# adaLN quarters of the first stage moved ahead of the latents' products of the round before

## The chip, the cores and the metric

The kernel runs on one core of a Trainium2 chip. A core has five engines that run side by side, each through a list of instructions in a fixed order: TensorE (PE) multiplies matrices, VectorE (DVE) and ScalarE (ACT) work on elements, GpSimd (POOL) has little to do here, and SyncE (SP) issues the loads from memory, which 16 DMA engines carry out. The metric is the device time of one launch in microseconds (us), as the median of several runs.

## The reference

The program is a decoder trunk of two layers for 256 tokens of width 1024, in float32. Each sub-layer is normalised, scaled and shifted by vectors that come from a conditioning vector c (adaLN). Only the start of the first layer matters here: the modulation, the normalisation and the first projection of the latent attention.

```python
cond = jax.nn.silu(c)
for i in range(DEPTH):
    mod = cond @ ada_w[i] + ada_b[i]
    sh1, sc1, g1, sh2, sc2, g2 = [m[:, None, :] for m in jnp.split(mod, N_MOD, axis=-1)]
    h = rms_norm(x, norm_mix[i]) * (1.0 + sc1) + sh1
    # layer 0: latent attention
    proj = h @ w_in                                  # 1024 x (512 + 256 + 32)
    q_lat, kv_lat, k_rope = jnp.split(proj, [Q_LORA, Q_LORA + KV_LORA], axis=-1)
    q = (rms_norm(q_lat, q_norm) @ w_qb)
    kv = (rms_norm(kv_lat, kv_norm) @ w_kvb)
```

The gates, the dense feed-forward layer, the gated delta layer and the experts come after that, in the same way in both kernels.

## The kernel before

**Halves.** Products are made from float32 numbers cut in two: a high half in a reduced format and the rest. A weight slab is loaded by a DMA into one of 10 ring tiles (`wload`, L182; tile `w`), copied into its high half by ScalarE (CAST, tile `whi`, L463) and the rest is found by VectorE (subtraction, tile `wlo`, L468); `Flow.split` (L454) issues both. There are four tiles for `whi` and four for `wlo`. Each block product is three matmuls: high by high, high by low, low by high (L885 to L887), so the third reads `wlo`.

**Stage and rounds.** The first stage works in four rounds (i = 0 to 3, `mla`, L871). Round i treats a quarter of the model width, 256 columns, which is two of the eight blocks of 128. The shift sh1 and the scale sc1 of these columns are made by an adaLN quarter: 4 loads of 512 KB (`ada_load`, L630; those of h = 1 of quarter 3 go to a pool of their own, tile `adaw`), two halves of 8 products each with the conditioning vector as stationary operand (`ada_half`, L647, products at L652; the profile counts 16 instructions), a copy from PSUM by VectorE (`adarow`, L657), two transposes (L659), and then, on VectorE, column sums (`half`, `mod`, `scl`, L664 to L668). `norm_blocks` (L373) then writes the two blocks of the normalised input: `nt` (VectorE, L378), its high half `hhi` (ScalarE, L382), its low half `hlo` (VectorE, L389).

The latents' weights of a round are two slabs, 288 KB for kv (with the rotary key) and 512 KB for q. `latents(i, "kv")` makes 18 products from the first slab, `latents(i, "q")` 24 from the second (`latents`, L877), all summed in PSUM banks over the four rounds.

**Order.** The order on TensorE, VectorE, ScalarE and GpSimd is the order in which the program calls; nothing reorders it. SP's order is the order of `loads` with `load_to` (L643), where a load waits until its ring tile is free and until the load eight places earlier has landed. In a round the kernel before splits the round's two slabs first, then makes the two halves of the quarter, and weaves the products of the round before between them: kv behind the first half, q behind the quarter's transposes. Between the rounds VectorE works at the tables of the rotary embedding (`rope_steps`, nine steps at a time). After the fourth round come the products of round 3, then the latents' own norms (`ss`, `r`) and the projections to heads. The name k0 stands for the first slab of those (slab 8 of the flow), q0 for the next (slab 9).

Of the kernel before, what the change touches and what calls it, by code (L numbers as in the profile page):

```python
# [23 lines left out]
AHEAD = 6  # L24
# [25 lines left out]
def hybrid_kernel(ctx: ExitStack, tc: tile.TileContext, rope_rows, x, c, positions, ada_w, ada_b,  # L50
# [31 lines left out]
    def acc_bank(name="acc"):  # L82
        return banks["pool"].tile([128, 512], F32, name=name, tag="acc", bufs=banks["acc"])
# [88 lines left out]
    def rope_steps(n):  # L172
        for _ in range(n):
            next(rope, None)
# [7 lines left out]
    def wload(srcs, shape, name="w"):  # L182
        raw = (ring[0]() if ring else wrw).tile(shape, F32, name=name, tag="w")
        for dst, src in srcs(raw):
            nc.sync.dma_start(dst, src)
        return raw
# [177 lines left out]
    def in_rows(r, bank):  # L364

        pb = bank("rb")
        for t in range(2):
            nc.tensor.transpose(pb[:, t * 128:(t + 1) * 128], r[:, t:t + 1].to_broadcast([128, 128]), ident)
        return pb[:, :S]
# [3 lines left out]
    def norm_blocks(layer, which, blocks, r, hi, lo, share=(), depth=1):  # L373
        late = []
        for i in blocks:
            t = sm.tile([128, S], F32, name="nt", tag="sq", bufs=4)
            sh = modT[layer, 3 * which][:, i:i + 1]
            nc.vector.scalar_tensor_tensor(t, in0=xT[:, i, :], scalar=scl[layer, which][:, i:i + 1],  # L378
                                           in1=r, op0=OP.mult, op1=OP.mult)
            if len(late) == depth:  # L380
                late.pop(0)()
            nc.scalar.activation(hi[:, i, :], t, AF.Identity, bias=sh)  # L382

            def low(i=i, t=t, sh=sh):
                if i in share:
                    nc.scalar.activation(t, t, AF.Identity, bias=sh)
                    nc.gpsimd.tensor_tensor(lo[:, i, :], t, hi[:, i, :].bitcast(F32), op=OP.subtract)
                else:
                    nc.vector.scalar_tensor_tensor(lo[:, i, :], in0=t, scalar=sh, in1=hi[:, i, :].bitcast(F32),  # L389
                                                   op0=OP.add, op1=OP.subtract)  # L390

            late.append(low)
        for low in late:
            low()
# [177 lines left out]
    for t in range(2):  # L572
        q = sm.tile([128, D], F32, name="xsq", tag="xsq", bufs=1)
# [37 lines left out]
    for name in GROUPS_T:  # L611
        t, i = int(name[1]), len(slabs)
# [10 lines left out]
    flow = Flow(slabs, uses, lambda i: False, 3)  # L623
# [4 lines left out]
    ada_raw, loads = {}, []  # L628

    def ada_load(i, h, m):  # L630
        wv = ada_w[0].rearrange("(k p) c -> p k c", p=128)[:, 4 * h:4 * h + 4, m * D + i * S:m * D + (i + 1) * S]
        if (i, h) == (3, 1):
            raw = adp.tile([128, D], F32, name="adaw", tag="w").rearrange("p (k c) -> p k c", k=4)
            nc.sync.dma_start(raw, wv)
        else:
            raw = wload(lambda t: [(t, wv)], [128, 4, S])
        ada_raw[i, h, m] = raw

    for i in range(4):
        loads += [lambda i=i, h=h, m=m: ada_load(i, h, m) for h in range(2) for m in range(2)]  # L640
        loads += [lambda j=j: flow.load(j) for j in (2 * i, 2 * i + 1)]

    def load_to(n):  # L643
        while 24 - len(loads) < n:
            loads.pop(0)()

    def ada_half(i, h, ps):  # L647
        for k in range(4):
            for m in range(2):
                kk = 4 * h + k  # L650
                c = 64 * m + 32 * (k % 2)
                mm(ps[c:c + 32, :S], lhsT=csil[:, kk:kk + 1].to_broadcast([128, 32]),  # L652
                   rhs=ada_raw[i, h, m][:, k, :], start=kk < 2, stop=kk > 5, tile_position=(0, c))

    def ada_quarter(i, ps):
        row = adp.tile([128, S], F32, name="adarow", tag="row", bufs=1)
        nc.vector.tensor_copy(row, ps[:, :S])  # L657
        for cc in range(2):
            nc.tensor.transpose(ps[:, S + cc * 128:S + (cc + 1) * 128], row[:, cc * 128:(cc + 1) * 128], ident)  # L659
        c = slice(2 * i, 2 * i + 2)  # L660
        pv = ps[:, S:].rearrange("p (c m j r) -> p m c j r", c=2, m=2, j=2)[:, :, :, :, 0]
        for m in (1, 0):
            half = sm.tile([128, 2], F32, name="half", tag="half", bufs=2)
            nc.vector.tensor_tensor(half, pv[:, m, :, 0], adab[:, 0, m, c], op=OP.add)  # L664
            nc.vector.tensor_tensor(modT[0, m][:, c], pv[:, m, :, 1], half, op=OP.add)
            if m == 1:
                g = cols[:, col_of["nm"] + 2 * i:col_of["nm"] + 2 * i + 2]
                nc.vector.scalar_tensor_tensor(scl[0, 0][:, c], in0=modT[0, 1][:, c], scalar=1.0, in1=g,  # L668
                                               op0=OP.add, op1=OP.mult)
        norm_blocks(0, 0, (2 * i, 2 * i + 1), rx, hhi, hlo)  # L670
# [195 lines left out]
    def room(name):  # L866
        while waiting[0] > 2:
            flow.idle()
        return mm_bank(name)

    def mla():  # L871
# [5 lines left out]
        def latents(i, which):  # L877
            flow.begin()
            for k, (h, l) in enumerate(flow.slab[2 * i + (which == "q")]):
                kk = 2 * i + k  # L880
                rh, rl = hhi[:, kk, :], hlo[:, kk, :]
                for j, (bank, b) in enumerate(place[which]):
                    o = bank[:, b * S:(b + 1) * S]
                    c = slice(160, 288) if which == "kv" and j == 2 else slice(j * 128, (j + 1) * 128)
                    mm(o, lhsT=h[:, c], rhs=rh, start=kk == 0 and b == 0, stop=False, skip_group_check=True)  # L885
                    mm(o, lhsT=h[:, c], rhs=rl, start=False, stop=False, skip_group_check=True)
                    mm(o, lhsT=l[:, c], rhs=rh, start=False, stop=kk == 7, skip_group_check=True)  # L887
            flow.advance()

        load_to(10)  # L890
        for i in range(4):
            flow.split(True)
            flow.split(True)
            load_to(min(24, 12 + 6 * i))
            ps = ada_bank[i % 2]
            for h in range(2):
                ada_half(i, h, ps)
                if i == h == 0:
                    nc.scalar.copy(rx, in_rows(xr, acc_bank))
                load_to(min(24, 14 + 6 * i + 2 * h))  # L900
                if i == 3 and h:
                    flow.load(9)
                    flow.ahead = AHEAD
                    flow.split(True)
                if h:
                    ada_quarter(i, ps)
                if i:
                    latents(i - 1, ("kv", "q")[h])
            rope_steps(9)

        def out_of(which, j):
            bank, b = place[which][j]
            return bank[:, b * S:(b + 1) * S]
# [24 lines left out]
        for name in GROUPS_T:  # L938
            t, i = int(name[1]), at[name]
            if name[0] == "k":  # L940
                ps = room("k")
# [8 lines left out]
                ps = room("v")  # L950
# [12 lines left out]
            else:  # L963
                for u in range(3):
                    ps = room("qr") if u == 0 else ps if u == 2 else room("q")
# [52 lines left out]
    for i, _ in enumerate(mla()):  # L1018
        if i > 4:
            next(pair, None)  # L1020
# [42 lines left out]
    flow = ffn_flow  # L1063
# [133 lines left out]
    flow = gdn_flow  # L1197
# [521 lines left out]
    ps = acc_bank("pos")  # L1719
# [511 lines left out]
```

## Time and profile before

| | us |
|---|---|
| median of 3 runs | 995.1 (992.34 to 997.79) |
| the profiled execution | 997.03 |
| its span, first to last instruction | 995.3 |
| TensorE busy | 931.6 (94%) |
| VectorE busy | 671.4 (67%) |
| ScalarE busy | 486.2 (49%) |
| mean granted clock of TensorE | 0.963 of full speed |

Times in the trace count from the start of the span. A row of the timeline is one instruction or a run of equal ones; in square brackets stand how long its engine had been idle before it and what released it. Matmuls are pipelined, so the distance of their starts says more than their durations: 0.28 us is the duration of a product of 256 columns, but the next one starts 0.12 us later. The granted clock is a share of TensorE's full 2.4 GHz; it is either 0.5 or 1, and a stretch in between mixes both. The DMA share is the mean busy share of the 16 DMA engines; packets overlap, so it can pass 1.

### The profile page before, as it was taken

How to read it: one execution, taken by the hardware profiler on the slowest of the kernel's cores; microseconds unless marked ns; L12 is line 12 of the kernel's file. 1: busy time of each engine (PE TensorE's matmuls, PEld its weight loads, DVE VectorE, ACT ScalarE, POOL GpSimd, SP SyncE). 2: the span in 40 equal slices, each digit the busy share in tenths (PEclk: the TensorE clock that was granted, in tenths of full speed). 3: DMA queues.
4: the chain of work that ended last, by engine and by line, in shares of the span. 5: the costliest groups of instructions: out<-in, count | busy, mean ns of one | idle time of the engine just before them, and what ended most of it. 6: DMA issues, size and time to landing. Idle time of an engine off the chain costs nothing. (4 is left out here: it accounts for less than half of the span.)

```text
span 995.3 us, 18930 instructions
## 1 busy us (share of the span) xinstructions
PE 931.6 (94%) x6802; PEld 749.5 (75%) x6802; DVE 671.4 (67%) x1281; ACT 486.2 (49%) x877; POOL 123.7 (12%) x226
## 2 busy tenths in 40 slices
PE   5899999999999999899999989899989999999995
PEld 3787888999999989789889877755774567356642
DVE  5778957877777768977764458925872488257532
ACT  2366646444444457544563366723662366236422
POOL 2000001000000024535663240000000000000000
PEclk7999998999999989899999979999999999999998
DMA  9959995979988955432223365979999999999992
GB/s 308 366 178 315 303 288 167 312 238 338 312 285 293 304 163 179 140 107 86 86 86 101 113 212 175 318 259 370 365 394 370 363 353 342 382 358 367 364 372 71
DMA packets 152741, 261.34 MB, mean 263 GB/s; under 512 B 13650, under 2 KB 104832, under 8 KB 152640
## 3 DMA queue, kind: packets, MB, share of 16 engines
q1 hardware_dynamic: 152336, 259.81, 76.3%
q8 instruction: 55, 0.90, 0.4%
q0 software_dynamic: 304, 0.25, 0.1%
q14 instruction: 46, 0.38, 0.1%
HBM read 258.97 MB, written 1.05 MB: 261 GB/s over the span
## 5 line engine op out<-in xcount | busy, mean ns | idle before, releaser
L463 ACT CAST whi<-w 128x1024 fp32r<-128x1024 f32 (+3 forms) x147 | 138.6, 958 | 115.4 <-PE gu L1145 45.0
L200 DVE TENSOR_TENSOR wlo<-w,whi 128x1024 fp32r<-128x1024 f32 (+1 forms) x136 | 153.0, 1155 | 33.8 <-ACT whi L199 32.1
L468 DVE TENSOR_TENSOR wlo<-w,whi 128x1024 fp32r<-128x1024 f32 (+3 forms) x132 | 147.9, 1135 | 21.6 <-ACT whi L463 21.2
L199 ACT CAST whi<-w 128x1024 fp32r<-128x1024 f32 (+1 forms) x136 | 131.8, 998 | 35.7 <-PE gu L2069 18.5
L1144 PE MATMUL gu<-hhi,whi 128*128 128x256 f32 x336 | 95.4, 284 | 0.0
L1146 PE MATMUL gu<-hhi,wlo 128*128 128x256 f32 x336 | 95.1, 283 | 0.0
L1145 PE MATMUL gu<-hlo,whi 128*128 128x256 f32 x336 | 95.1, 283 | 0.0
L2099 PE MATMUL gu<-w,XF 128*64 128x512 f32 (+1 forms) x384 | 85.3, 564 | 0.0
L232 PE MATMUL pj<-hhi,whi 128*128 128x256 f32 x240 | 73.6, 307 | 0.0
L234 PE MATMUL pj<-hhi,wlo 128*128 128x256 f32 x240 | 68.5, 286 | 3.8 <-DVE wlo L468 3.8
L233 PE MATMUL pj<-hlo,whi 128*128 128x256 f32 x240 | 68.4, 285 | 0.0
L468 POOL TENSOR_TENSOR wlo<-w,whi 128x1024 fp32r<-128x1024 f32 x15 | 39.3, 2622 | 226.3 <-DVE al L1119 181.2
L1145 PEld LDWEIGHTS gu<-hlo,whi 128*128 128x128 f32 x336 | 64.5, 192 | 0.0
L1144 PEld LDWEIGHTS gu<-hhi,whi 128*128 128x128 f32 x336 | 64.5, 192 | 0.0
L1146 PEld LDWEIGHTS gu<-hhi,wlo 128*128 128x128 f32 x336 | 64.5, 192 | 0.0
L2069 PE MATMUL gu<-whi,XH 128*128 128x512 f32 x192 | 59.4, 390 | 3.6 <-ACT whi L199 3.4
L2069 PE MATMUL gu<-wlo,XH 128*128 128x512 f32 x192 | 59.7, 392 | 2.2 <-DVE wlo L200 2.2
L2099 PEld LDWEIGHTS gu<-w,XF 128*64 128x64 f32 x384 | 26.4, 136 | 44.5 <-issue 39.5
L2069 PE MATMUL gu<-whi,XL 128*128 128x512 f32 x192 | 58.2, 385 | 0.0
L262 DVE SCALAR_TENSOR_TENSOR adacc<-adaw,csil,adacc 128x1024 f32<-128x1024 f32 x42 | 56.1, 1336 | 2.2 <-DMA adaw<-in_ada_w_dram 2.2
L1106 PE MATMUL acc<-ah,whi 128*128 128x256 f32 x176 | 50.0, 284 | 0.0
L1107 PE MATMUL acc<-al,whi 128*128 128x256 f32 x176 | 49.8, 283 | 0.0
(526 smaller groups left out, 2213.0 us busy)
## 6 DMA issues: line engine op xcount, KB each, us to landing
w<-in_moe_w_down_dram SPq DMA_DIRECT2D x84, 512.0 KB, 6.8
w<-in_moe_w_gate_up_dram SPq DMA_DIRECT2D x128, 256.0 KB, 5.4
w<-in_moe_w_gate_up_dram SPq DMA_DIRECT2D x64, 512.0 KB, 6.9
adaw<-in_ada_w_dram SPq DMA_DIRECT2D x50, 512.0 KB, 5.3
w<-in_moe_w_gate_up_dram SPq DMA_DIRECT2D x128, 192.0 KB, 4.0
w<-in_ada_w_dram SPq DMA_DIRECT2D x46, 512.0 KB, 6.6
w<-in_ffn_w_gate_up_dram SPq DMA_DIRECT2D x88, 256.0 KB, 5.5
w<-in_gdn_w_in_dram SPq DMA_DIRECT2D x32, 512.0 KB, 4.6
```

Of the source, the lines that this page charges most:

```text
L199: nc.scalar.copy(dv(hi), rv(raw))
L200: eng.tensor_tensor(dv(lo), rv(raw), dv(hi).bitcast(F32), op=OP.subtract)
L232: mm(ps, lhsT=lhi, rhs=rhi, start=first, stop=False)
L233: mm(ps, lhsT=lhi, rhs=rlo, start=False, stop=False)
L234: mm(ps, lhsT=llo, rhs=rhi, start=False, stop=last)
L463: nc.scalar.copy(dv(hi), rv(raw))
L468: eng.tensor_tensor(dv(lo), rv(raw), dv(hi).bitcast(F32), op=OP.subtract)
L1144: mm(o, lhsT=h[:, c], rhs=rh, start=k == g == 0 and new, stop=False, skip_group_check=True)
L1145: mm(o, lhsT=h[:, c], rhs=rl, start=False, stop=False, skip_group_check=True)
L1146: mm(o, lhsT=l[:, c], rhs=rh, start=False, stop=k == 1 and g == 3, skip_group_check=True)
L2069: mm(p[:, :2 * m].rearrange("p (g c) -> p g c", g=2), lhsT=x[:, kk, :], rhs=w[:, k, :, o:o + m], start=kk == i == 0, stop=kk == 7 and i == 2)
L2099: mm(o, lhsT=X[:, k, :], rhs=r, start=k == 0, stop=k == 7, tile_position=(0, 64 * h))
```

## The change

The list of loads is written out: quarter 0, weights 0, quarter 1, quarter 2, weights 1, quarter 3, weights 2, weights 3, where before each quarter was followed by the weights of its own round. The split of a pair of slabs moves too. Weights 0 are split at the start; weights 1 behind quarter 2, weights 2 behind quarter 3, weights 3 after the loop. The products of the round before no longer stand between the halves of a quarter (but for kv of round 0, which stays between the halves of quarter 1): in rounds 2 and 3 both halves and the transposes come first, then the split, then kv and q. The split of k0 and the loads ahead of it move from the middle of round 3 to after the loop.

```diff
-    for i in range(4):
-        loads += [lambda i=i, h=h, m=m: ada_load(i, h, m) for h in range(2) for m in range(2)]
-        loads += [lambda j=j: flow.load(j) for j in (2 * i, 2 * i + 1)]
+    for what, i in (("a", 0), ("w", 0), ("a", 1), ("a", 2), ("w", 1), ("a", 3), ("w", 2), ("w", 3)):
+        if what == "a":
+            loads += [lambda i=i, h=h, m=m: ada_load(i, h, m) for h in range(2) for m in range(2)]
+        else:
+            loads += [lambda j=j: flow.load(j) for j in (2 * i, 2 * i + 1)]
...
         load_to(10)
-        for i in range(4):
+
+        def weights():
             flow.split(True)
             flow.split(True)
+
+        weights()
+        for i in range(4):
             load_to(min(24, 12 + 6 * i))
             ps = ada_bank[i % 2]
             for h in range(2):
...
                 load_to(min(24, 14 + 6 * i + 2 * h))
-                if i == 3 and h:
-                    flow.load(9)
-                    flow.ahead = AHEAD
-                    flow.split(True)
-                if h:
-                    ada_quarter(i, ps)
-                if i:
-                    latents(i - 1, ("kv", "q")[h])
+                if i == 1 and h == 0:
+                    latents(0, "kv")
+            ada_quarter(i, ps)
+            if i > 1:
+                weights()
+                latents(i - 1, "kv")
+            if i:
+                latents(i - 1, "q")
             rope_steps(9)
+        weights()
+        flow.load(9)
+        flow.ahead = AHEAD
+        flow.split(True)
```

TensorE around quarter 2, before: the end of the kv products of round 1, the second half of the quarter, its transposes, and the q products of round 1. The names in brackets are semaphores, DMAHW those of loads, DVE and Activation those of VectorE and ScalarE.

```order
L885 MATMUL lat<-hhi,whi 128x256
L886 MATMUL lat<-hlo,whi 128x256
L887 MATMUL lat<-hhi,wlo 128x256
L652 MATMUL ada<-w,csil 32x256 [waits DMAHW0_49]
L652 MATMUL ada<-w,csil 32x256 [waits DMAHW1_49]
L652 MATMUL ada<-w,csil 32x256 x6
L659 MATMUL ada<-ident,adarow 128x128 [waits DVE_49]
L659 MATMUL ada<-ident,adarow 128x128
L885 MATMUL lat<-hhi,whi 128x256
L886 MATMUL lat<-hlo,whi 128x256
L887 MATMUL lat<-hhi,wlo 128x256
```

The same place after: the last products before it are those of q of round 0, and behind the transposes stand kv of round 1.

```order
L889 MATMUL lat<-hhi,wlo 128x256
L654 MATMUL ada<-w,csil 32x256 [waits DMAHW4_49]
L654 MATMUL ada<-w,csil 32x256 [waits DMAHW5_49]
L654 MATMUL ada<-w,csil 32x256 x6
L654 MATMUL ada<-w,csil 32x256 [waits DMAHW6_49]
L654 MATMUL ada<-w,csil 32x256 [waits DMAHW7_49]
L654 MATMUL ada<-w,csil 32x256 x6
L661 MATMUL ada<-ident,adarow 128x128 [waits DVE_49]
L661 MATMUL ada<-ident,adarow 128x128
L887 MATMUL lat<-hhi,whi 128x256 [waits Activation_49]
L888 MATMUL lat<-hlo,whi 128x256
L889 MATMUL lat<-hhi,wlo 128x256 [waits DVE_49]
```

Both halves now stand together, and the first and the third product behind the transposes wait for ScalarE and VectorE, where before none of them waited.

VectorE around quarter 2, before: weights 2 are split ahead of the quarter's `adarow`, weights 3 behind its `hlo`.

```order
L468 TENSOR_TENSOR wlo<-w,whi 128x576 [waits DMAHW2_49,Activation_49]
L468 TENSOR_TENSOR wlo<-w,whi 128x1024 [waits DMAHW3_49,PE_49,Activation_49]
L657 COPY adarow<-ada 128x256 [waits PE_49]
L664 TENSOR_TENSOR half<-ada,adab 128x2 [waits PE_49]
L665 TENSOR_TENSOR mod_125<-ada,half 128x2 [waits DVE_49]
L668 SCALAR_TENSOR_TENSOR scl_136<-mod_125,cols 128x2 [waits DVE_49]
L664 TENSOR_TENSOR half<-ada,adab 128x2
L665 TENSOR_TENSOR mod_124<-ada,half 128x2 [waits DVE_49]
L378 SCALAR_TENSOR_TENSOR nt<-xT,scl_136,rx 128x256 x2
L389 SCALAR_TENSOR_TENSOR hlo<-nt,mod_124,hhi 128x256 [waits Activation_49] x2
L468 TENSOR_TENSOR wlo<-w,whi 128x576 [waits DMAHW0_49,Activation_49]
L468 TENSOR_TENSOR wlo<-w,whi 128x1024 [waits DMAHW1_49,PE_49,Activation_49]
```

The same place after: the quarter, and behind it the split of weights 1.

```order
L659 COPY adarow<-ada 128x256 [waits PE_49]
L666 TENSOR_TENSOR half<-ada,adab 128x2 [waits PE_49]
L667 TENSOR_TENSOR mod_125<-ada,half 128x2 [waits DVE_49]
L670 SCALAR_TENSOR_TENSOR scl_136<-mod_125,cols 128x2 [waits DVE_49]
L666 TENSOR_TENSOR half<-ada,adab 128x2
L667 TENSOR_TENSOR mod_124<-ada,half 128x2 [waits DVE_49]
L378 SCALAR_TENSOR_TENSOR nt<-xT,scl_136,rx 128x256 x2
L389 SCALAR_TENSOR_TENSOR hlo<-nt,mod_124,hhi 128x256 [waits Activation_49] x2
L468 TENSOR_TENSOR wlo<-w,whi 128x576 [waits DMAHW0_49,Activation_49]
L468 TENSOR_TENSOR wlo<-w,whi 128x1024 [waits DMAHW1_49,Activation_49]
```

The rows are the same instructions in the same order, but the subtraction behind the quarter is now that of the slabs whose products stand next on TensorE.

## Rows read from the trace of the kernel before

**Rows 1.** Stretches: us, busy time of each engine, granted clock, DMA share, GB/s

```profile
15.00:25.00 10.00, 8.05 (x55) 3.68 (x48) 8.61 (x24) 3.57 (x6) 0.00 (x0) 0.50 1.09 356
...
30.00:35.00 5.00, 5.00 (x50) 4.28 (x49) 3.87 (x13) 1.88 (x5) 0.00 (x0) 1.00 1.08 359
...
55.00:60.00 5.00, 5.00 (x47) 5.00 (x45) 3.40 (x15) 3.48 (x10) 0.00 (x0) 1.00 0.34 129
```

**Rows 2.** Timeline of TensorE, end of the stage: start, us, instruction [idle before]

```profile
55.15 0.28 PE L887 MATMUL lat<-hhi,wlo 128*128 128x256 f32 x1
55.27 0.95 PE L344 MATMUL ss<-ones,lsq 128*128 128x1 f32 x8
```

**Rows 3.** Timeline of round 1, TensorE and VectorE

```profile
27.11 1.07 PE L652 MATMUL ada<-w,csil 128*32 128x256 f32 x16
27.45 1.89 DVE L468 TENSOR_TENSOR wlo<-w,whi 128x576 fp32r<-128x576 f32 x2
...
29.25 0.42 DVE L657 COPY adarow<-ada 128x256 f32<-128x256 f32 x1
...
29.73 0.44 PE L659 MATMUL ada<-ident,adarow 128*128 128x128 f32 x2 [1.55 <-DVE adarow L657]
```

**Rows 4.** Timeline of round 2, TensorE, VectorE and ScalarE

```profile
36.30 1.07 PE L652 MATMUL ada<-w,csil 128*32 128x256 f32 x16
...
37.69 0.42 DVE L657 COPY adarow<-ada 128x256 f32<-128x256 f32 x1
...
38.16 0.44 PE L659 MATMUL ada<-ident,adarow 128*128 128x128 f32 x2 [0.80 <-DVE adarow L657]
...
38.68 0.28 PE L887 MATMUL lat<-hhi,wlo 128*128 128x256 f32 x1
...
39.88 0.91 ACT L382 ACTIVATE hhi<-nt,mod 128x256 fp32r<-128x256 f32 x2 [3.36 <-DVE nt L378]
...
40.42 0.89 DVE L389 SCALAR_TENSOR_TENSOR hlo<-nt,mod,hhi 128x256 fp32r<-128x256 f32 x2 [0.18 <-ACT hhi L382]
...
40.69 0.66 ACT L463 CAST whi<-w 128x576 fp32r<-128x576 f32 x1
...
41.38 0.76 DVE L468 TENSOR_TENSOR wlo<-w,whi 128x576 fp32r<-128x576 f32 x1
...
42.01 1.05 ACT L463 CAST whi<-w 128x1024 fp32r<-128x1024 f32 x1 [0.66 <-DMA w<-in_mla_w_in_dram]
...
43.09 1.23 DVE L468 TENSOR_TENSOR wlo<-w,whi 128x1024 fp32r<-128x1024 f32 x1 [0.95 <-ACT whi L463]
```

**Rows 5.** Timeline of round 3, VectorE and TensorE

```profile
45.42 1.29 DVE L468 TENSOR_TENSOR wlo<-w,whi 128x512 fp32r<-128x512 f32 x2 [1.10 <-ACT whi L463]
...
47.11 0.44 PE L659 MATMUL ada<-ident,adarow 128*128 128x128 f32 x2 [1.30 <-DVE adarow L657]
```

**Rows 6.** Waits from 15 to 56 us (total, times, longest); stretches from the start

```profile
PEld ada L652 <- issue: 1.8, 7, 0.3
...
0.00:30.00 30.00, 16.89 (x109) 10.59 (x109) 18.34 (x55) 8.38 (x13) 6.54 (x19) 0.77 0.98 315
...
0.00:40.00 40.00, 26.09 (x198) 18.28 (x199) 25.78 (x78) 11.90 (x20) 6.54 (x19) 0.83 1.00 326
```

**Rows 7.** Timeline of TensorE behind the stage, and the clock there

```profile
59.17 1.84 PE L344 MATMUL ss<-ones,lsq 128*128 128x1 f32 x16
63.32 0.40 PE L368 MATMUL rb<-ident,r 128*128 128x128 f32 x2 [2.31 <-DVE r L320]
...
64.20 0.41 PE L234 MATMUL qr<-lat_h,wlo 128*128 128x256 f32 x1
...
67.41 0.32 PE L234 MATMUL q<-lat_h,wlo 128*128 128x256 f32 x1
...
64.20:67.00 2.80, 2.80 (x15) 2.80 (x15) 2.65 (x8) 2.77 (x7) 0.00 (x0) 0.50 0.02 1
```

**Rows 8.** Waits of SP's own queue from 56 to 160 us

```profile
SPq L185 <- DVE wlo L468: 31.7, 9, 7.1
```

## The prediction

> **What bounds the kernel now.** The page first: TensorE is busy for 94% of the span, so what is worth time is the moments in which it has nothing to do. The change touches the first stage alone, the 56 us in which the latents' input weights and the first two adaLN vectors are loaded and multiplied. I read the stretches of that stage next [rows 1]: from 15 to 25 us the loads run without a pause (DMA share 1.09) and TensorE is at 0.50 of its clock, 1.2 GHz, the lower of its two levels; from 30 to 60 us the granted clock is 1.00, 2.4 GHz, the upper level (six stretches of 5 us, of which the first and the last stand there), and TensorE is filled but for short waits; after 55 us the DMA share is down to 0.34. The stage ends for TensorE with the last product of the latents at 55.15, and the sums of squares start right behind it [rows 2]. Everything later hangs on that product.
>
> Is that end set by the loads or by a chain of engines? The last slab of the latents' weights is copied into its high half at 42.01, after a wait of 0.66 us for its load [rows 4], and its products end 13 us later. So the loads are done with this stage long before TensorE is. What is left between the products are the quarters of adaLN. A quarter is: two halves of adaLN products (call them H, 1.07 us each), a copy by VectorE (adarow), two transposes by TensorE (call them T), then columns, modulation and normalisation on VectorE and ScalarE, which give hhi and hlo for two blocks of the latents' input. In round 2 this chain is undisturbed: H from 36.30, adarow 37.69, T at 38.16 after a wait of 0.80, hhi from 39.88, hlo from 40.42 and 0.89 long [rows 4]. In round 1 adarow comes behind two wlo subtractions (27.45, together 1.89 us) and T waits 1.55 [rows 3]; in round 3 behind two others (45.42) and T waits 1.30 [rows 5]. While the chain behind T runs, TensorE always has products of the round before, whose weights were split long ago: in round 2 the third product after T starts at 38.68, 0.52 us after T [rows 4]. That cover is what the change takes away.
>
> **The change part by part.** *Loads.* No byte is added; quarters 2 and 3 move ahead of weight pairs 1 and 2. What this can bring is bounded by how long H waits for its data now: from 15 us on H lost 1.8 us in 7 pieces of at most 0.3 us, none of them to a load [rows 6]. So an earlier quarter buys nothing by itself. Does anything come too late? The new order has, up to quarter 2, x 1.05 MB, small rows 0.26, quarters 3 x 2.10 and one weight pair 0.82: 8.4 MB; up to quarter 3, 11.35 MB; up to the last pair, 13.0 MB as before. The mean rates [rows 6] give 315 x 30 = 9.45 MB by 30 us and 326 x 40 = 13.0 MB by 40 us, so quarter 2 is there near 28 us, quarter 3 near 36, and both are wanted later than that (33 and 44 us, below). SP's queue only meets buffers freed by H one round before. Cost: 0.
>
> *Round 1.* The two wlo subtractions no longer stand in front of adarow. T then waits as in round 2: 0.80 in place of 1.55, **-0.75 us**. Round 3 likewise loses what stood in front of its adarow (1.30 to 0.80), **-0.50 us**.
>
> *Rounds 2 and 3, behind T.* Here the order on VectorE and ScalarE decides. The products that follow T are now those of the pair of weights that is split only after the quarter (weights 1 behind quarter 2, weights 2 behind quarter 3): the CAST stands behind both hhi, the subtraction behind both hlo. Queued behind the waiting product on TensorE are all other products of the stage, the next H among them. The rows of before hold exactly this sequence, since in round 2 the last weights' split stands behind the quarter: T 38.16, hlo until 41.31, CAST 40.69 to 41.35, wlo 41.38 to 42.14 [rows 4]. So wlo is done 3.98 us after T starts, and the third product, which reads it, starts then and not 0.52 us after T: **+3.46 us** a round, two rounds, **+6.9 us**. The second slab's copy and subtraction (1.05 and 1.23 us) are hidden by the 18 kv products (18 x 0.12 = 2.1 us) behind which its first product stands. Bounds of this term: if only the CAST were waited for, 41.35 - 38.16 - 0.2 = 3.0 a round, 6.0 in all; if the second slab were late as well, about 0.4 a round more, 7.7 in all. I take the sequence as the rows have it.
>
> The sum of the waits: 6.9 - 0.75 - 0.5 = **+5.7 us**. By hand: T of quarter 1 at 28.98; 24 products, two H and a wait of 0.80 bring T of quarter 2 to 35.1; the third kv product follows at 39.1; 40 products, two H and 0.80 later T of quarter 3 at 47.0 and its third product at 51.0; then 82 products of 0.12, that is an end near 60.9 in place of 55.3.
>
> *The clock.* Each of the new stretches is a wait of 0.80, the short T, and a wait of 3 us with two products in it. What does such a stretch do? The nearest row is at 59 to 63 us: after sums over a single column (59.17) TensorE waited 2.31 us for a reciprocal root, and from 64.20 its products were 0.21 apart, at a granted clock of 0.50, until 67.41 [rows 7]. That is 15 products in 3.2 us that take 1.8 at 0.12: 1.4 lost. The waits of 1.55 and 1.30 left the clock at 1.00 [rows 1, 3, 5]. The new stretch is longer than all three and emptier, so I take a fall after each, with 1.5 us lost each, **+3.0 us**. Bounds: 0, and all 42 products of a round at 0.21, 42 x 0.09 = 3.8 a round, 7.6 in all.
>
> *What lies behind.* The splits of the first two slabs of the next stage come later but keep their place before the last latents' products; they need tiles that the kv and q products of round 3 free, as before. Loads behind the stage wait for tiles that splits set free (31.7 us in 9 waits on wlo from 56 us on, [rows 8]), so they shift with the splits and absorb nothing. 0, with the whole shift passed on.
>
> The sum is 5.7 + 3.0 = **+8.7 us**. The profiled execution took 997.0 (span 995.3) and would take 1005.7; the median of the three runs of before is 995.1, so I forecast **1003.8**.
>
> **The rivals.** *A, the waits come but the clock holds.* For it: two waits of 1.3 to 1.55 us cost no clock [rows 3, 5]. Against it: the 2.31 us wait did [rows 7]. It gives 995.1 + 5.7 = 1000.8. The Trainium skill's page "Perfetto Trace Analysis", section "Matmul Optimizations", asks for products back to back in batches because the engine follows its utilisation; the change does join two H and then 42 products. By that rule the change would gain clock, and its sum would at best be the 5.7 without the 3.0; the trace has 1.00 from 30 to 60 us, with nothing left to gain, so I keep the 3.0.
>
> *B, the loads set the end and nothing changes.* The DMA share is 1.08 to 1.09 in the stretches shown up to 35 us [rows 1], and if the stage's end followed the last load, an order of loads with the same last byte would give 995.1 again. The place is the last weight pair; it decides if the products end within some 3 us of its landing. They end 13 us after it [rows 2, 4]. The Trainium skill's page "Perfetto Trace Analysis", section "Identifying the Most-Contended Engine", says that improving a kernel generally means improving its most contended engine, which would here be the DMA; that is this rival, and the 13 us speak against it. The same time comes out if a later stage swallows the shift, against which stands [rows 8].
>
> *C, not slower: only the gains of rounds 1 and 3 are left.* It needs the first wlo of weights 1 and 2 to be done by the time T ends, which holds if the split stands ahead of the quarter's hlo on VectorE. Then 995.1 - 1.25 = 993.9. Against it: in the new order the subtraction stands behind hlo on VectorE, and that engine takes its rows in order.
>
> *D, the clock stays low for whole rounds.* From 15 to 25 us, with TensorE busy for 8.05 of the 10 us, it was 0.50 throughout [rows 1]. Then 995.1 + 5.7 + 7.6 = 1008.4.
>
> **How the numbers follow.** Forecast 0.63, A 0.13, B 0.10, C 0.04, D 0.10. A measurement of this kernel can tell some 0.5%, 5 us, from no change, so A at 1000.8 is just over that bound and I count two thirds of it as slower. Slower: 0.63 + 0.09 + 0.10 = 0.82; same: 0.04 + 0.10 + 0.02 of C = 0.16; faster 0.02. The range: from A with a shift 1.8 us smaller than summed, 999.0, to D, 1009.0; B and C are left out.
>
> **What the profile after would show.** T of quarter 1 waits about 0.8 us. Behind T of quarters 2 and 3 the third product waits for wlo, T to product near 4.0 us, VectorE busy all that time with the quarter. The last product of the latents ends near 61 us with the clock held, 64 without. Granted clock 0.50 in a stretch behind each wait. H has no wait for a load. From there on every line lies 5 to 9 us later, at the same distances. Wrong would be: the last product near 55 us (then B or C), H waiting for loads, or a later stage that ends at its old time.

## The result and the profile after

The changed kernel takes **1003.98 us** in the median (1002.96 to 1007.1, six runs), the kernel before 996.0 in the runs beside it; the ratio is 1.0084 with an interval of 1.0069 to 1.0100. It is slower by 8 us. The profiled executions have spans of 1005.4 and 995.3.

The rows behind quarter 2 in the trace after answer to [rows 4]. First TensorE's timeline (start, us, instruction, idle before it): the second half H and the transposes T of quarter 1, then T of quarter 2 and the first products behind it.

```profile
27.50 1.07 PE L654 MATMUL ada<-w,csil 128*32 128x256 f32 x16
29.14 0.45 PE L661 MATMUL ada<-ident,adarow 128*128 128x128 f32 x2 [0.57 <-DVE adarow L659]
...
34.89 0.44 PE L661 MATMUL ada<-ident,adarow 128*128 128x128 f32 x2 [0.57 <-DVE adarow L659]
38.13 0.58 PE L887 MATMUL lat<-hhi,whi 128*128 128x256 f32 x1 [2.80 <-ACT whi L463]
38.51 0.41 PE L888 MATMUL lat<-hlo,whi 128*128 128x256 f32 x1
38.92 0.58 PE L889 MATMUL lat<-hhi,wlo 128*128 128x256 f32 x1
39.30 0.41 PE L887 MATMUL lat<-hhi,whi 128*128 128x256 f32 x1
39.52 0.41 PE L888 MATMUL lat<-hlo,whi 128*128 128x256 f32 x1
```

TensorE stands still for 2.80 us until ScalarE has copied the high half, and the third product starts 4.03 us after T, where it was 0.52 before. From there the products are 0.21 apart and not 0.12. What ScalarE and VectorE did meanwhile, from the whole timeline:

```profile
36.61 0.91 ACT L382 ACTIVATE hhi<-nt,mod 128x256 fp32r<-128x256 f32 x2 [2.19 <-DVE nt L378]
37.15 0.89 DVE L389 SCALAR_TENSOR_TENSOR hlo<-nt,mod,hhi 128x256 fp32r<-128x256 f32 x2 [0.18 <-ACT hhi L382]
37.42 1.60 ACT L463 CAST whi<-w 128x576 fp32r<-128x576 f32 x2
38.11 0.76 DVE L468 TENSOR_TENSOR wlo<-w,whi 128x576 fp32r<-128x576 f32 x1
```

The copy and the subtraction of weights 1 stand behind hhi and hlo of quarter 2, without a pause between them. No load is late here; the place of the split in the two lists makes the wait. Round 3 repeats it to the hundredth: T, first and third product.

```profile
48.71 0.44 PE L661 MATMUL ada<-ident,adarow 128*128 128x128 f32 x2 [0.57 <-DVE adarow L659]
51.95 0.58 PE L887 MATMUL lat<-hhi,whi 128*128 128x256 f32 x1 [2.80 <-ACT whi L463]
...
52.74 0.58 PE L889 MATMUL lat<-hhi,wlo 128*128 128x256 f32 x1
```

The stage's end, which answers to [rows 2], and the wait for the reciprocal root behind it, which answers to [rows 7]:

```profile
64.91 0.95 PE L344 MATMUL ss<-ones,lsq 128*128 128x1 f32 x8
...
72.95 0.66 PE L368 MATMUL rb<-ident,r 128*128 128x128 f32 x2 [2.31 <-DVE r L320]
```

Both lie 9.6 us later than before (55.27 and 63.32). Of this, 0.4 us was there ahead of every product that the change moves behind quarter 1: the second half H of that quarter starts at 27.50 here and at 27.11 in the profile before [rows 3]. Two kernels below whose program is the same up to there, vec_delay and one_round, have 27.94 and 26.94, so it varies from profile to profile. Stretches after (us, busy time of PE, PEld, DVE, ACT and POOL, granted clock, DMA share, GB/s) show the clock: full ahead of quarter 2's transposes, half behind each of the two waits, full between them and after the second stretch.

```profile
30.00:34.00 4.00, 4.00 (x53) 3.19 (x51) 3.54 (x11) 1.46 (x4) 0.00 (x0) 1.00 1.09 350
38.20:43.80 5.60, 5.60 (x25) 5.31 (x26) 1.89 (x2) 0.82 (x1) 0.00 (x0) 0.50 1.06 380
46.00:50.00 4.00, 2.58 (x37) 1.21 (x35) 1.13 (x7) 0.00 (x0) 0.00 (x0) 1.00 0.32 92
51.90:57.40 5.50, 5.45 (x24) 5.16 (x25) 4.19 (x5) 3.52 (x5) 0.00 (x0) 0.50 0.66 221
58.00:64.90 6.90, 6.90 (x60) 6.90 (x59) 2.19 (x5) 2.95 (x8) 0.00 (x0) 1.00 0.93 309
73.60:77.80 4.20, 4.20 (x22) 4.20 (x21) 4.06 (x10) 4.07 (x9) 0.00 (x0) 0.50 0.00 0
```

The DMA share falls to 0.32 at 46 us: the loads of this stage are through, while TensorE still has quarter 3 and the 84 products of rounds 2 and 3 to do.

### The profile page after: what moved, and what is told of

It reads as the page before. It is cut to its first block, busy times and chain, and to the rows that moved or that the text cites. A ratio compares the mean times of both kernels' runs of the same rounds, so it can differ in the third digit from the quotient of the medians.

```text
span 1005.4 us, 18930 instructions
## 1 busy us (share of the span) xinstructions
PE 937.8 (93%) x6802; PEld 755.0 (75%) x6802; DVE 671.2 (67%) x1281; ACT 486.3 (48%) x877; POOL 123.7 (12%) x226
## 5 line engine op out<-in xcount | busy, mean ns | idle before, releaser
L234 PEld LDWEIGHTS pj<-hhi,wlo 128*128 128x128 f32 x240 | 46.9, 195 | 4.1 <-DVE wlo L468 4.1
```

The lines of the kernel that those rows point to most:

```text
L234: mm(ps, lhsT=llo, rhs=rhi, start=False, stop=last)
```

## The experiments

The theory is that the place of the split costs the time: behind the quarter it leaves TensorE without work, and the clock falls on top. The rivals are the order of the loads, the waits without the clock, and a loss elsewhere. "Stage end" is the start of the first `ss` row in the profiled execution: 55.27 before, 64.91 after. The ratio is taken to the runs of the kernel before that stood beside each kernel (medians 995.2 to 996.0).

| kernel | stage end, us | median, us | ratio to before (interval) |
|---|---|---|---|
| changed kernel | 64.91 | 1003.98 | 1.0084 (1.0069 to 1.0100) |
| order_only | 64.42 | 1003.43 | 1.0087 (1.0055 to 1.0119) |
| fill | 60.47 | 999.44 | 1.0032 (1.0013 to 1.0051) |
| one_round | 58.42 | 998.33 | 1.0032 (1.0015 to 1.0049) |
| vec_delay | 66.30 | 1005.2 | 1.0102 (1.0071 to 1.0133) |
| split_early | 55.68 | 995.88 | 1.0006 (0.9986 to 1.0026) |
| split_early_rope | 53.42, 53.26 | 991.73, 993.76 | 0.9955 (0.9938 to 0.9973), 0.9987 (0.9969 to 1.0006) |
| cover | 54.20 | 993.62 | 0.9978 (0.9963 to 0.9994) |
| cover_w2 | 51.79 | 991.66 | 0.9964 (0.9953 to 0.9975) |
| loads_only | 62.08 | 1003.21 | 1.0068 (1.0051 to 1.0085) |

**The order of the loads taken back (order_only).**

```diff
-    for what, i in (("a", 0), ("w", 0), ("a", 1), ("a", 2), ("w", 1), ("a", 3), ("w", 2), ("w", 3)):
...
+    for i in range(4):
+        loads += [lambda i=i, h=h, m=m: ada_load(i, h, m) for h in range(2) for m in range(2)]
+        loads += [lambda j=j: flow.load(j) for j in (2 * i, 2 * i + 1)]
```

> The changed kernel with the old order of loads (each quarter followed by the weights of its own round); splits and products stand as in the changed kernel. Theory 'split behind the quarter': the two new waits of TensorE and the falls of its clock come from the order on VectorE and ScalarE, so nothing changes against the changed kernel: 1004 us, 8 over the kernel before, third product 4.0 us after T in rounds 2 and 3. Theory 'order of loads': the loss comes from quarters and weights that are loaded at other times, so the old order gives the time of before, 996.

TensorE behind T of quarter 2:

```profile
34.63 0.44 PE L659 MATMUL ada<-ident,adarow 128*128 128x128 f32 x2 [0.57 <-DVE adarow L657]
37.87 0.58 PE L885 MATMUL lat<-hhi,whi 128*128 128x256 f32 x1 [2.80 <-ACT whi L463]
...
38.66 0.58 PE L887 MATMUL lat<-hhi,wlo 128*128 128x256 f32 x1
```

It measured 1003.43, with the same 2.80 us in front of the first product and the third one 4.03 us after T. The loss is there without the new order of loads.

**TensorE kept busy in the wait (fill).** The extra products change nothing that is computed.

```diff
                 weights()
+                for _ in range(28):
+                    mm(fill[:, :S], lhsT=hhi[:, 0, 0:128], rhs=hhi[:, 0, :], start=True, stop=True)
                 latents(i - 1, "kv")
```

> The changed kernel with 28 extra products of 256 columns (block 0 of the normalised input with itself, into a bank that nothing reads) behind the transposes of quarters 2 and 3, 3.4 us at the upper clock in a wait of some 3.8. Theory 'waits and clock': the waits stay (third product 4.0 us after T) but the clock stays at 1.00 from 30 to 65 us; the stage then ends near 60.3 where the changed kernel has 64.9, and the time is 1001, 4 under the changed kernel and 5 over the one before. Theory 'waits alone, the clock's fall is covered by other waits': 1004. If the extra products cost something themselves: over 1004.

TensorE's timeline with the filling products, two of its stretches, and the stage's end:

```profile
35.00 0.44 PE L661 MATMUL ada<-ident,adarow 128*128 128x128 f32 x2 [0.57 <-DVE adarow L659]
35.20 3.60 PE L914 MATMUL fill<-hhi 128*128 128x256 f32 x28
38.63 0.28 PE L888 MATMUL lat<-hhi,whi 128*128 128x256 f32 x1
38.75 0.28 PE L889 MATMUL lat<-hlo,whi 128*128 128x256 f32 x1
39.04 0.38 PE L890 MATMUL lat<-hhi,wlo 128*128 128x256 f32 x1
...
36.00:44.00 8.00, 7.99 (x66) 7.67 (x64) 3.92 (x9) 2.42 (x4) 0.00 (x0) 1.00 1.06 378
...
47.00:60.00 13.00, 12.99 (x109) 12.79 (x108) 9.28 (x19) 7.82 (x15) 0.00 (x0) 1.00 0.86 271
...
60.47 0.95 PE L344 MATMUL ss<-ones,lsq 128*128 128x1 f32 x8
```

The third product still starts 4.04 us after T, so the chain is as long as before; but the clock stays at 1.00 and the stage ends at 60.47, 4.4 us earlier than in the changed kernel. The median is 4.5 us lower (999.44, where 1001 was expected). So 4.4 of the 9.6 us are the clock. The other 5.2 hold a late start like the one above (H of quarter 1 ends 0.5 us later than before) and some 4.7 us of waits. The Trainium skill's page "Perfetto Trace Analysis", section "Matmul Optimizations", says that the matmul engine scales its power by its utilisation. The rows agree: 1.00 with the filling products, 0.50 without them. Products that nobody reads were enough.

**One of the two waits taken away (one_round).** Weights 2 are split at the end of round 2, weights 3 behind quarter 3.

```diff
             if i > 1:
                 weights()
...
+                if i == 2:
+                    latents(i - 1, "kv")
+                    latents(i - 1, "q")
+                    weights()
```

> The changed kernel with weights 2 and 3 split one round earlier (weights 2 at the end of round 2, weights 3 behind quarter 3), so that only the products behind quarter 2 wait for a split behind the quarter. Theory 'split behind the quarter': one wait of 3.5 us and one fall of the clock (some 2 us) are left, less about 2 us that the shorter waits for the copy of the sums gain: 999.5, half way. Theory that the loss lies elsewhere (halves that stand together, loads, a later stage): 1004 as in the changed kernel.

TensorE behind T of quarter 3, where the split now stands ahead of the quarter:

```profile
48.11 0.44 PE L661 MATMUL ada<-ident,adarow 128*128 128x128 f32 x2 [0.57 <-DVE adarow L659]
48.30 0.36 PE L887 MATMUL lat<-hhi,whi 128*128 128x256 f32 x1
48.50 0.28 PE L888 MATMUL lat<-hlo,whi 128*128 128x256 f32 x1
48.62 0.28 PE L889 MATMUL lat<-hhi,wlo 128*128 128x256 f32 x1
```

The third product is back at 0.51 us after T; the wait in round 2 is unchanged (2.80). The stage ends 6.5 us earlier than in the changed kernel. Of this, 0.6 us stood already at T of quarter 1 (28.58 here, 29.14 there), 3.5 are the wait, and the remaining 2.4 are the second fall of the clock. The median is 998.33, where 999.5 was expected.

**More VectorE work in the chain (vec_delay).** The added subtraction is not read.

```diff
             if i > 1:
+                xf = xT[:, 0:4, :].rearrange("p a t -> p (a t)")
+                nc.vector.tensor_tensor(fillv, xf, xf, op=OP.subtract)
                 weights()
```

> The changed kernel with one more VectorE subtraction of 128 x 1024 (1.23 us, result not read) between the low half of the normalised input and the split's subtraction, in rounds 2 and 3. Theory 'split behind the quarter': the chain on VectorE sets when TensorE goes on, so each is paid in full: the third product 5.2 us after T, stage 2.5 us longer, 1006.5 (1 us either way by where the clock falls). Theory that another wait, a load or ScalarE, ends TensorE's wait: 1004.

Now the wait ends with VectorE by the profile's own reckoning:

```profile
38.56 0.58 PE L888 MATMUL lat<-hhi,whi 128*128 128x256 f32 x1 [2.80 <-ACT whi L463]
40.33 0.58 PE L890 MATMUL lat<-hhi,wlo 128*128 128x256 f32 x1 [0.97 <-DVE wlo L468]
```

The third product starts 5.00 us after T, 0.97 later than in the changed kernel, and the stage ends 1.4 us later, not 2.5; the median rises by 1.2, not 2.5. The direction is as the theory has it, the size is about half. The traces account for it: T of quarter 1 was already 0.45 us later (29.59), the two longer waits cost 0.97 each, and behind them 19 and 15 products follow at 0.21 us, where the changed kernel has 23 and 22. These 11 fewer at 0.09 us give 1.0 back: 0.45 + 1.94 - 1.0 = 1.4. The expectation left that gain out.

**The split one round earlier (split_early).** Weights 1 are split behind quarter 1, and so on.

```diff
-            if i > 1:
+            if i:
                 weights()
+            if i > 1:
                 latents(i - 1, "kv")
...
-        weights()
```

> The changed kernel with each pair of weights split behind the quarter of its own round, one round earlier than in the changed kernel (weights 1 behind quarter 1 and so on); loads and products as in the changed kernel. The tables of the rotary embedding (1.8 us of VectorE) stay at the end of round 1, now behind that split. Theory 'split behind the quarter': the products behind T find their weights split, third product 0.5 us after T, no fall of the clock there. But VectorE reaches the copy of quarter 2 some 2 us late, so T of quarter 2 waits 2.4 us: stage end near 55.4, time 996 (up to 997.5 if the clock falls at that wait). Theory that halves standing together or the loads cost the time: 1004.

VectorE's timeline in rounds 1 and 2, T of quarter 2 and the third product behind it:

```profile
32.78 1.23 DVE L468 TENSOR_TENSOR wlo<-w,whi 128x1024 fp32r<-128x1024 f32 x1 [0.20 <-ACT whi L463]
33.93 0.88 DVE L161 SCALAR_TENSOR_TENSOR ang<-nn,ang 128x256 f32<-128x256 f32 x2
...
35.51 0.41 DVE L659 COPY adarow<-ada 128x256 f32<-128x256 f32 x1
...
35.98 0.44 PE L661 MATMUL ada<-ident,adarow 128*128 128x128 f32 x2 [2.20 <-DVE adarow L659]
...
36.49 0.38 PE L889 MATMUL lat<-hhi,wlo 128*128 128x256 f32 x1
```

The median is 995.88, and the third product starts 0.51 us after T. The loss is gone when the split moves, although the halves still stand together and the loads keep their new order. What is left is a wait of 2.20 in front of T, because the rotary tables (`ang`) stand ahead of `adarow`; the clock was at 0.50 behind it from 36.5 to 39.0.

**The rotary tables behind the rounds (split_early_rope, measured twice).**

```diff
-            rope_steps(9)
+            if i == 0:
+                rope_steps(9)
+        rope_steps(9)
```

> As the run before, with the rest of the rotary tables moved behind the four rounds. Theory 'split behind the quarter': T waits 0.6 to 0.9 us in rounds 1 to 3 and every product behind it finds its weights; clock 1.00 from 30 us on; stage end near 53.6, 1.7 us before that of the kernel before: 994.3. If the order of rows on VectorE ahead of the copy does not matter: as the run before.

> The version with early splits and late rotary tables once more, on the same chip as the run above, to compare the two: stage end 53.1 to 53.6, 991.7 (ratio 0.9955 before). If its lead over the kernel before was the phase of the clock in those runs, the ratio goes toward 0.998.

The stage ends at 53.42 and 53.26, 1.9 to 2.0 us before that of the kernel before, as worked out. The medians, 991.73 and 993.76, do not agree as well with each other: a ratio of 0.9955 in one set and 0.9987 in the other. In the second set's profile the first rounds ran earlier, and T of quarter 2 waited 1.78 us for `adarow` behind a split that had waited for its load. By the stage the version gains 2 us. Over the whole run the first set shows 4 us, and the second shows nothing clear of its interval, so the size of the gain stays open.

**Products between halves and transposes (cover).**

```diff
-            ada_quarter(i, ps)
-            if i > 1:
+            ada_quarter(i, ps, (lambda: latents(i - 1, "kv")) if i in (1, 2) else None)
+            if i == 3:
+                weights()
+                latents(2, "kv")
+            elif i:
                 weights()
```

> As the run before, with the kv products of the round before between the halves and the transposes of quarters 1 and 2, so that TensorE has work while VectorE copies the sums. Theory 'TensorE's empty moments in this stage set its end': two waits of 0.6 to 0.9 us go, stage end near 52, 3.3 us before that of the kernel before: 992.5. Rival: the loads now set the pace (quarter 3 lands near 37.5, the last weights near 42): stage end 53.6, 994.3.

The stage ends at 54.20, not at the expected 52. The timeline of round 3 says why:

```profile
39.85 1.04 ACT L463 CAST whi<-w 128x1024 fp32r<-128x1024 f32 x1 [0.69 <-DMA w<-in_mla_w_in_dram]
...
40.93 1.23 DVE L468 TENSOR_TENSOR wlo<-w,whi 128x1024 fp32r<-128x1024 f32 x1 [0.98 <-ACT whi L463]
42.07 0.42 DVE L659 COPY adarow<-ada 128x256 f32<-128x256 f32 x1
...
42.55 0.69 PE L663 MATMUL ada<-ident,adarow 128*128 128x128 f32 x2 [2.51 <-DVE adarow L659]
```

The copy of quarter 3 stands behind the subtraction of weights 2, which waits for their load. TensorE reaches quarter 3 early enough here for a load to be late.

**Weights 2 loaded ahead of quarter 3 (cover_w2).**

```diff
-(("a", 0), ("w", 0), ("a", 1), ("a", 2), ("w", 1), ("a", 3), ("w", 2), ("w", 3))
+(("a", 0), ("w", 0), ("a", 1), ("a", 2), ("w", 1), ("w", 2), ("a", 3), ("w", 3))
```

> The kernel with kv products between halves and transposes of quarters 1 and 2, with weights 2 loaded ahead of quarter 3. In the run before this one T of quarter 3 waited 2.5 us: its copy stood on VectorE behind the subtraction of weights 2, which waited for their load at 39.8. Theory 'the load of weights 2 is what was late': with the pair landed near 34 the copy is free, the second half of quarter 3 waits under 1 us for its own load (near 39.8), T of quarter 3 starts near 41.5 and the stage ends near 52 at the upper clock, 2 us before the run before: 992. Rival: the last loads of quarter 3 only take over as what is late (T after 42.5, clock falls): 993.6 as before. Against the version with early splits and late rotary tables (991.7) a difference under 2 us is within what five rounds can tell.

```profile
39.73 1.06 PE L654 MATMUL ada<-adaw,csil 128*32 128x256 f32 x14 [0.47 <-DMA adaw<-in_ada_w_dram]
41.36 0.44 PE L663 MATMUL ada<-ident,adarow 128*128 128x128 f32 x2 [0.56 <-DVE adarow L659]
```

T of quarter 3 at 41.36, stage end 51.79, 991.66 us, ratio 0.9964 (0.9953 to 0.9975): as expected, and clear of both kernels. It has the earliest stage end here, and its median is 3.5 us under that of the kernel before in the same set and 12 under the changed kernel's. Its lead over split_early_rope in that set (993.76) is 2.1 us, about the 2 us that the expectation called the limit of what can be told.

**The loads alone (loads_only).** The kernel before with the changed list of loads.

> The kernel before with the new order of loads alone. Weights 1 land some 6 us later, while their split still stands ahead of quarter 1 on ScalarE and VectorE. Theory 'what stands in front on VectorE and ScalarE sets TensorE's waits': the copy of quarter 1 stands behind a subtraction that waits for that load, T of quarter 1 starts near 34 and not 29.7, with a fall of the clock behind it: stage end near 60, 1001. Theory 'loads ahead of need cost nothing': 996.

```profile
31.57 1.04 ACT L463 CAST whi<-w 128x1024 fp32r<-128x1024 f32 x1 [1.36 <-DMA w<-in_mla_w_in_dram]
32.65 1.23 DVE L468 TENSOR_TENSOR wlo<-w,whi 128x1024 fp32r<-128x1024 f32 x1 [1.64 <-ACT whi L463]
33.79 0.42 DVE L659 COPY adarow<-ada 128x256 f32<-128x256 f32 x1
34.26 0.69 PE L661 MATMUL ada<-ident,adarow 128*128 128x128 f32 x2 [6.15 <-DVE adarow L659]
```

T of quarter 1 starts at 34.26 after a wait of 6.15, the stage ends at 62.08 (60 expected) and the median is 1003.21 (1001 expected). So the new loads do not go with a split ahead of quarter 1. They do go with a split behind it (split_early, no loss); the change splits one quarter later still, and that costs. The costs of the two halves do not add up: the loads alone cost about 7 us, the new places of splits and products alone about 8 (order_only), and both together 8. The halves of the change cannot be judged one by one from the kernel before.

## Why the prediction was right, point by point

The forecast was 1003.8 and the measured time 1003.98. The mechanism held: the waits stand where they were forecast, and the clock falls behind each. That the two times agree to 0.2 us is luck. The waits were summed 0.6 us too large and the clock 1.4 us too small, the base of 995.1 was 0.9 us under the 996.0 measured beside the change, and the medians differ by 8.0 us where 8.7 were forecast.

*Loads, cost 0.* Right, with the split where the change has it: order_only gives the time of the changed kernel, and no half of a quarter waited for a load in it.

*Round 1 and round 3, -0.75 and -0.50.* Too small. I took the wait of 0.80 in round 2 for the undisturbed chain. It was not undisturbed: there too adarow (37.69) started only when a subtraction of weights 2 ended. The chain alone makes T wait 0.57, in all three rounds after. The gain is 0.98 + 0.23 + 0.73 = 1.94, not 1.25.

*Behind T, +3.46 a round.* Right: 4.03 - 0.52 = 3.51, twice, 7.0. With the line above, the waits come to 7.0 - 1.9 = 5.1, against 5.7 forecast. Fill shows 60.47 - 55.27 = 5.2, or about 4.7 without its late start.

*The clock, +3.0.* The mechanism was right, the size too small: 4.4 by fill against the changed kernel. The nearest row had 15 products at the lower level; here there were some 25 each time (5.6 and 5.5 us at 0.50), which at 0.09 us lost on each is 2.2 a fall. The bound of 3.8 a round held.

*What lies behind, the whole shift passed on.* Right as far as the trace goes: 9.6 us at 64.91 and at 72.95, 10.1 at the end of the span, though the prediction expected 5 to 9 there. The medians differ by 8.0 and the stages by 9.6; the profiled execution of the changed kernel was the slowest of its six (1007.1). The interval of the ratio allows 6.9 to 10.0 us, so these runs cannot tell the two apart.

*The rivals.* A (clock holds) is fill, not the change. B fell: the loads ended long before the stage. C named the right condition: with the weights split before the quarter in question (split_early_rope), 991.73 and 993.76 were measured, where C had 993.9. D, the clock low for whole rounds, did not come.

## What to carry to other kernels

When products are moved, ask what each engine's list holds between the last thing they need and the first thing they wait for: a step that was covered by products of an earlier round costs its whole chain once those products need something issued behind it. Split or prepare operands one round before they are used, and keep work without a deadline (here the rotary tables) out of the lists that a waiting engine hangs on. A wait on TensorE can be paid for twice: here each added 3.5 us, and the lower clock behind it about 2.2 us more. Price both, and check by filling the wait.

## What had not been expected of the hardware

The clock of the first 25 us is not the same in every execution of the same work. In the profile of split_early the stretch from 15 to 25 us stands at 1.00, where that of the kernel before had 0.50 [rows 1] with the same busy time of TensorE:

```profile
15.00:25.00 10.00, 8.05 (x56) 3.70 (x49) 8.62 (x24) 2.90 (x5) 0.00 (x0) 1.00 1.09 350
```

T of quarter 1 then stood at 28.60, against 29.14 in the changed kernel, which ran that stretch at 0.50. The same kernel shows it too: of the two profiles of split_early_rope one has 0.50 in this stretch and the other 0.83, with T of quarter 1 at 29.04 and 27.63. And behind the same wait of 2.31 us for the reciprocal root the clock was low for some 3 us, until 67.4, in the profile before [rows 7], and for over 4 us, past 77.8, in the one after. So the same work gets a different clock from one execution to another; how much of the spread of the runs (991 to 999 us for the kernel before) comes from it was not measured.
